# Block products behind gating products, zero matmuls at the head, split column parameters and a later mean square in a two-block kernel

## Chip, cores and metric

The kernel runs on one core of one Trainium2 chip, as one launch. The metric is the device time of the execution in microseconds (us), as the median of the runs shown. Engines are named as the profile names them: PE is TensorE (PEld its weight loads), DVE VectorE, ACT ScalarE, POOL GpSimd, SP SyncE.

## The reference, cut to what matters

Two blocks run one after the other on 256 positions of width 1024, in float32. The first is a mixer of four branches and then a gated FFN with a causal convolution; the second has an S5 branch, an mLSTM branch and a retrieval FFN. The change touches the start of the first block, its FFN, and the preparation of the second block's constants.

```python
def rms_norm(x, g):
    xf = x.astype(jnp.float32)
    y = xf * lax.rsqrt(jnp.mean(xf * xf, axis=-1, keepdims=True) + RMS_EPS)
    return (y * g.astype(jnp.float32)).astype(x.dtype)
...
def first_block(...):
    for l in range(DEPTH):
        h = rms_norm(x, mix_norm_g[l])
        x = x + hybrid_mixer(h, w_in[l], ...)
        h = rms_norm(x, ffn_norm_g[l])
        x = x + conv_glu_ffn(h, w_up[l], ffn_conv_w[l], w_down[l])
    return rms_norm(x, final_norm_g)
...
def conv_glu_ffn(h, w_up, conv_w, w_down):
    up = causal_dwconv(h @ w_up, conv_w)
    gate, val = jnp.split(up, 2, axis=-1)
    return (jax.nn.silu(gate) * val) @ w_down
...
def s5_branch(u, a_re, a_im, log_dt, b_re, b_im, c_re, c_im, d, w_glu, b_glu):
    lam = lax.complex(a_re.astype(f32), a_im.astype(f32))
    dt = jnp.exp(log_dt.astype(f32))[:, None]
    a_bar = jnp.exp(lam * dt)
    b_bar = ((a_bar - 1.0) / lam)[..., None] * lax.complex(b_re.astype(f32), b_im.astype(f32))
    ...
```

The products of `a_bar` with the matrices B and C depend on parameters alone. The kernel multiplies them out for four steps in advance, while the first block's FFN runs.

## The kernel before, in words

Channels lie on partitions, positions along the free axis. Every matrix product keeps float32 precision by three matmuls: weights and activations are each split into a rounded high part and a rest, and `mm3` (L405 to L407) multiplies high by high, high weight by rest, and rest of the weight by high. Weights come in units of eight 128x128 tiles (512 KB). A unit is loaded by SP, its high part `wh` is cast by ACT (L339) and its rest `wl` is subtracted by DVE (L340), up to three units ahead of TensorE.

At the head, the eight channel tiles of X arrive in four loads, with the column parameters `cols` (one 128x286 table) between them. `pre` (L434, L435) scales and splits them into `h`; `square` makes the squares, which POOL sums (L444). The eight z blocks of the rwkv branch are the first products (L405 to L407, out `z`). After the second one, `rstd` (L453) sums the squares over partitions with two matmuls by ones; the scale is applied to z afterwards, in `shift`.

The FFN (`up` and `down`) has 22 steps. `up(i)` makes 48 matmuls into two banks `u`, convolves on ACT and DVE (L1888 to L1890), takes the Silu on ACT (L1891) and multiplies gate by value on POOL (L1892, the gating product; the last three are on DVE). In the next step `split` (L429 on ACT, L430 on DVE) makes `ffnr` from the product, and `down(i - DN)` multiplies it by the down weights with 24 matmuls (L1903 to L1905, out `acc`). So a step has 72 matmuls.

`_prep` is a generator that runs beside the FFN: `tick`, called for each weight unit, lets it issue a little more. Its block products (`paced`, L564) are 48 tensor_tensors of 128x512 on POOL, with a negation at L575 and one at L583. TensorE transposes their results (`pt`, L591), ACT evicts the transposes (L592), and further matmuls (`pk`, L599) follow. Then come eight folds of the mLSTM's matrices: three expands each on POOL (L492) and three small matmuls (`pf`, L639 to L641).

Each engine executes its instructions in its own fixed order. A scheduler derives that order when the program is built; `issue_after(ins)` adds an edge that keeps an instruction behind `ins` on the same engine, and `K.behind` uses that to hold background work behind a unit's cast, split and last matmul:

```python
def step(self, gen, lag):
    if len(self.splits) <= lag:
        return next(gen, None)
    with self.behind(lag):
        return next(gen, None)
```

Of the kernel before, what the change touches and what calls it, by code (L numbers as in the profile page):

```python
# [11 lines left out]
F16 = mybir.dt.float16  # L12
U32 = mybir.dt.uint32
AF = mybir.ActivationFunctionType
ALU = mybir.AluOpType
# [3 lines left out]
P = 128  # L19
D = 1024  # L20
T1 = 256
# [3 lines left out]
NFF = DFF // P  # L25
# [213 lines left out]
class _Space:  # L239


    def __init__(self, t):
        self.t, self.at = t, 0
# [21 lines left out]
class _K:  # L265
    def __init__(self, ctx, tc, I):
        self.tc, self.nc, self.I = tc, tc.nc, I
        self.misc = ctx.enter_context(tc.tile_pool(name="misc", bufs=1))
        self.bigp = ctx.enter_context(tc.tile_pool(name="big", bufs=8))
        self.g8p = ctx.enter_context(tc.tile_pool(name="g8", bufs=3))  # L270
        self.wp = ctx.enter_context(tc.tile_pool(name="w", bufs=4))
        self.dram = ctx.enter_context(tc.tile_pool(name="dram", bufs=1, space=bass.MemoryType.DRAM))
        self.pl = ctx.enter_context(tc.tile_pool(name="pl", bufs=4, space=PSUM))
        self.banks = ctx.enter_context(ExitStack())
        self.pm = self.banks.enter_context(tc.tile_pool(name="pm", bufs=4, space=PSUM))
        self.src = [I["W"][u] for u in range(N_UNITS)] + [I["U"][i] for i in range(NE)] + [I["V"][i] for i in range(NE)]
        self.raw, self.units, self.done = [], {}, 0
        self.at = -1
        self.bg, self.credit, self.rate = [], 0.0, RATE
        self.splits, self.last = [], None  # L280
        self.n = 0

    def name(self, s):
# [64 lines left out]
    def behind(self, lag=0):  # L348
# [4 lines left out]
                s.enter_context(self.tc.issue_after(ins))  # L353
        return s

    def step(self, gen, lag):
        if len(self.splits) <= lag:
            return next(gen, None)
        with self.behind(lag):
            return next(gen, None)  # L360
# [45 lines left out]
        mm(out, wh, al, start=False, stop=False)  # L406
        self.last = mm(out, wl, ah, start=False, stop=last).ins  # L407

    def lin(self, seg, i0, kt, hi, lo, out):

        for k in range(kt):
            wh, wl = self.w(seg, i0 + k)
            self.mm3(out, wh, wl, hi(k), lo(k), k == 0, k == kt - 1)

    def lin_nat(self, seg, hi, lo, outs, tsl, n2=2, kt=8, i0=0):

        mm = self.nc.tensor.matmul
        for k in range(kt):
            b = SEG_BASE[seg] + i0 + k * n2
            wh, wl, j = self.unit(b)  # L420
            rh = wh[:, j:j + n2].rearrange("p a b -> p (a b)")
            rl = wl[:, j:j + n2].rearrange("p a b -> p (a b)")
            for o, s in zip(outs, tsl):
                mm(o, hi(k)[:, s], rh, start=k == 0, stop=False)
                mm(o, hi(k)[:, s], rl, start=False, stop=False)
                mm(o, lo(k)[:, s], rh, start=False, stop=k == kt - 1)
# [18 lines left out]
        else:  # L445
            self.part[1] = s

    def rstd(self):

        nc = self.nc  # L450
        ms = self.ps("ms")[:, :T1]
        for i, s in enumerate(self.part):
            nc.tensor.matmul(ms, self.ones, s, start=i == 0, stop=i == 1)  # L453
        rs = self.misc.tile([P, T2], F32, name=self.name("rs"), tag="rs")
        nc.scalar.activation(rs[:, :T1], ms, AF.Sqrt, bias=self.eps, scale=1.0 / D)
        nc.vector.reciprocal(rs[:, :T1], rs[:, :T1])
        return rs[:, :T1]
# [10 lines left out]
def _prep(K, dump):  # L468

    nc, I, cols = K.nc, K.I, K.cols  # L470
    g = nc.gpsimd
    act, mm, tp = nc.scalar.activation, nc.tensor.matmul, nc.tensor.transpose
    tt, ts, stt = nc.vector.tensor_tensor, nc.vector.tensor_scalar, nc.vector.scalar_tensor_tensor
    EW, CX, TT, ZZ, BX = (K.big(f"s5{i}") for i in range(5))
    ew = EW.a(16, 2, P)
    cx = [CX.a(16, 4, 32) for _ in range(2)]
# [8 lines left out]
    ex = M5.a(3, P)  # L485
    msk = mp[:, 481:513]
    wif = mp[:, 288:480].rearrange("p (a b) -> p a b", b=8)
    wk, wv, rep, tr = mp[:, 0:32], mp[:, 32:64], mp[:, 64:192], [mp[:, 192 + 32 * i:224 + 32 * i] for i in range(3)]

    def expand(w, e, dst):  # L490

        g.tensor_tensor(dst.rearrange("p (a b) -> p a b", b=4), _bc(w[:, 4 * e:4 * e + 4], 1, 32), _bc(msk, 2, 4), ALU.mult)  # L492
# [10 lines left out]
    nc0, dk = (raw[:, 48 + 512 * i:560 + 512 * i].rearrange("p (a b) -> p a b", a=16) for i in range(2))  # L503
    x1, x2, kk = (ZZ.t[:, 2112 + 512 * i:2624 + 512 * i].rearrange("p (a b) -> p a b", a=16) for i in range(3))
    c0 = [TT.t[:, 2048 + 512 * i:2560 + 512 * i].rearrange("p (a b) -> p a b", a=16) for i in range(2)]
# [6 lines left out]
    dt, rho, th, n, r, sn, cs_, hs, den, kr, ki, u, w = v[:13]  # L512
# [46 lines left out]
    def paced(dr, di, xr_, xi, yr, yi):  # L559

        ops = []
        cmul(dr, di, xr_, xi, yr, yi, x1, x2, lambda *z: ops.append(z))
        for n, z in enumerate(ops):
            g.tensor_tensor(*z)  # L564
            if n not in (0, 3):
                yield 0.1

# [4 lines left out]
    for t in (2, 1, 0):  # L572
        yield from paced(bx[0][:, :, t], bx[1][:, :, t], bx[0][:, :, t + 1], bx[1][:, :, t + 1], bar, bai)
    yield from paced(c0[0], c0[1], C[:, 0], C[:, 1], bc(kr), bc(ki))
    g.tensor_scalar(nc0, c0[1], -1.0, None, ALU.mult)  # L575

    def outputs():
        pr, pi_ = c0
        for t in range(4):
            qr, qi = cx[0][:, :, t], cx[1][:, :, t]  # L580
            yield from paced(qr, qi, pr, pi_, bar, bai)
            pr, pi_ = qr, qi
        g.tensor_scalar(cx[1], cx[1], -1.0, None, ALU.mult)  # L583

    def inputs():

# [45 lines left out]
    nc.vector.tensor_reduce(nqk, pr4.rearrange("p (m d) -> p m d", d=4), AX.X, ALU.add)  # L632

    for e in range(8):
        for i in range(3):
            expand(tr[i], e, ex[:, i])
        yield 0.3
        pf = K.ps("pf")
        mm(pf[:, 0:8], ex[:, 0], wif[:, e], start=True, stop=False)  # L639
        mm(pf[:, 0:8], ex[:, 1], wif[:, 8 + e], start=False, stop=True)  # L640
        mm(pf[:, 8:16], ex[:, 2], wif[:, 16 + e], start=True, stop=True)  # L641
        nc.scalar.copy(fold[:, :, e], pf[:, 0:16].rearrange("p (a b) -> p a b", a=2))
# [691 lines left out]
def trainium_kernel(ctx, tc, I, O, dump=None, stop=None):  # L1334
    nc = tc.nc
    K = _K(ctx, tc, I)
    dump = dump or (lambda n, a: None)
    act, stt, tt, ts = nc.scalar.activation, nc.vector.scalar_tensor_tensor, nc.vector.tensor_tensor, nc.vector.tensor_scalar
# [7 lines left out]
    eps = K.misc.tile([P, 2], F32, name="eps")  # L1346
    nc.vector.memset(eps[:, 0:1], 1e-6)
    nc.vector.memset(eps[:, 1:2], 64e-5)
    act(K.misc.tile([P, 2], F32, name="warm"), eps, AF.Copy)
    for a, b in ((0, 1), (1, 2), (2, 4), (4, 8)):  # L1350
        nc.sync.dma_start(xr[:, a:b], I["xT"][:, a:b])
        if a == 0:
            nc.sync.dma_start(cols, I["cols"])
            K.load(1)
        if a == 1:
            K.piece(1)
    nc.sync.dma_start(eye2, I["eye"])
    ident, K.ones, K.iota, K.row0 = eye2[:, :P], eye2[:, P:2 * P], eye2[:, 2 * P:3 * P], eye2[:, 3 * P:]
    K.ident = ident
# [22 lines left out]
    h0, l0 = (lambda k: hi0[:, k]), (lambda k: lo0[:, k])  # L1382
# [39 lines left out]
        act(zp[:, n], zz[:, n, 1:T1 + 1], AF.Copy, scale=omu[:, n:n + 1])  # L1422
        stt(zp[:, n], zz[:, n, 0:T1], col("rw_mu", n), zp[:, n], ALU.mult, ALU.add)

    wait = []
    for j, n in enumerate(RW_ORDER):
        p = K.ps("z")
        K.lin("rw", j * 8, 8, h0, l0, p[:, :T1])
        wait.append((n, p[:, :T1]))
        if j == 1:  # L1430
            rs = K.rstd()
            nrm = K.start(K.normed(xr, COL["mix_norm_g"], rs, hi1, lo1, T1))
        if j:
            for w in wait:
                shift(*w)
            wait = []
# [243 lines left out]
    rw = K.start(rwkv())  # L1680
# [5 lines left out]
    for n in range(4):  # L1686
        p = K.ps("q")
# [59 lines left out]
    for n in range(2):  # L1747
        p = K.ps("u")
# [64 lines left out]
    for b in BR_ORDER[:3]:  # L1813
        g = mg if b == 0 else gc
# [4 lines left out]
        for m in range(4):  # L1819
            p = K.ps("br")  # L1820
# [34 lines left out]
    for n in range(8):  # L1855
        p = K.ps("o")
# [9 lines left out]
    h0, l0 = (lambda k: hi0[:, k]), (lambda k: lo0[:, k, :T1])  # L1866
# [4 lines left out]
    def up(i):  # L1871
        nonlocal rs, nrm, prep
        u, raw = ua[i % 4], i < RAW
        if i == RAW:
            K.finish(nrm)
        ps = [K.ps("u"), K.ps("u")]
        for e in range(2):
            K.lin(f"up{i}", e * 8, 8, h0 if raw else hh, l0 if raw else hl, ps[e][:, :T1])
            if i == 0 and e == 1:
                rs = K.rstd()  # L1880
                nrm = K.start(K.normed(xr, COL["ffn_norm_g"], rs, hi1, lo1, T1))
                prep = K.start(_prep(K, dump))
            for f in (0, 1) if i == 0 and e else (e,) if i else ():
                v, n = ps[f][:, :T1], f * NFF + i
                if raw:
                    tt(uv[:, f], v, rs, ALU.mult)
                    v = uv[:, f]
                act(u[:, f], v, AF.Copy, scale=col("ffn_conv_w", 2 * 44 + n))  # L1888
                stt(u[:, f, 1:], v[:, :T1 - 1], col("ffn_conv_w", 44 + n), u[:, f, 1:], ALU.mult, ALU.add)
                stt(u[:, f, 2:], v[:, :T1 - 2], col("ffn_conv_w", n), u[:, f, 2:], ALU.mult, ALU.add)  # L1890
        act(u[:, 0], u[:, 0], AF.Silu)  # L1891
        (nc.gpsimd.tensor_tensor if i < NFF - 3 else tt)(u[:, 0], u[:, 0], u[:, 1], ALU.mult)  # L1892
        if i > 0 and i <= NFF - 3:
            K.split(*uh[(i - 1) % 4], ua[(i - 1) % 4][:, 0])
        if i >= NFF - 3:
            K.split(*uh[i % 4], u[:, 0])
# [77 lines left out]
```

## Time and profile before

| | |
|---|---|
| median of 3 runs | 1595.97 us (1594.9 to 1597.15) |
| the profiled execution | 1592.86 us |
| its span, first to last instruction | 1591.0 us |
| mean granted TensorE clock | 0.987 |
| TensorE busy | 1535.2 us, 96%, 11661 matmuls |
| VectorE busy | 1146.4 us, 72% |
| ScalarE busy | 832.5 us, 52% |
| GpSimd busy | 237.4 us, 15% |
| the chain that ended last | PE 84%, POOL 7%, DVE 6%, ACT 1% |
| the FFN's gating products on POOL | 305.4 to 505.2 us |

The profile is of one execution. A row of a timeline has the start in us, the duration, the engine, the line, the operation, its output and inputs, the shape and a count; in brackets stands how long the engine had been idle before it and what released it. A row of a wait says which engine and line waited for which, the total in us, how often, and the longest. The granted clock is given as a share of full speed. A duration of a matmul covers its whole passage; matmuls are pipelined, so the time that one costs is the distance between two starts.

### The profile page before, as it was taken

How to read it: one execution, taken by the hardware profiler on the slowest of the kernel's cores; microseconds unless marked ns; L12 is line 12 of the kernel's file. 1: busy time of each engine (PE TensorE's matmuls, PEld its weight loads, DVE VectorE, ACT ScalarE, POOL GpSimd, SP SyncE). 2: the span in 40 equal slices, each digit the busy share in tenths (PEclk: the TensorE clock that was granted, in tenths of full speed). 3: DMA queues.
4: the chain of work that ended last, by engine and by line, in shares of the span. 5: the costliest groups of instructions: out<-in, count | busy, mean ns of one | idle time of the engine just before them, and what ended most of it. 6: DMA issues, size and time to landing. Idle time of an engine off the chain costs nothing.

```text
span 1591.0 us, 29719 instructions
## 1 busy us (share of the span) xinstructions
PE 1535.2 (96%) x11661; PEld 1425.3 (90%) x11661; DVE 1146.4 (72%) x2164; ACT 832.5 (52%) x1439; POOL 237.4 (15%) x254
## 2 busy tenths in 40 slices
PE   7999999987599999999999999999999999999998
PEld 7999899987599997889999999999999888888886
DVE  7765467865477788668899888788999566566664
ACT  7654345744345556555554554544444555555554
POOL 2000000275613002000100431112222000000000
PEclk9999999998899999999999999999999999999999
DMA  7543245544255553245545555555545556556563
GB/s 258 160 136 119 80 133 173 193 146 136 91 174 163 171 166 111 93 134 167 190 159 183 177 158 186 161 161 170 159 160 165 185 194 196 191 195 192 193 197 107
DMA packets 80717, 257.94 MB, mean 162 GB/s; under 512 B 17345, under 2 KB 18881, under 8 KB 80322
## 3 DMA queue, kind: packets, MB, share of 16 engines
q1 hardware_dynamic: 69200, 247.32, 48.3%
q10 hardware_dynamic: 11378, 8.73, 1.9%
q8 instruction: 92, 1.51, 0.4%
q14 instruction: 47, 0.39, 0.1%
HBM read 253.23 MB, written 2.13 MB: 161 GB/s over the span
## 4 chain that ended last, share of the span: by engine, by line
PE 84%; POOL 7%; DVE 6%; ACT 1%; issue 1%; DMA 1%; SPq 0%; ACTq 0%; POOLq 0%; DVEq 0%
PE acc L1297 22%; PE U L405 7%; PE U L407 6%; PE U L406 6%; POOL s L564 4%; PE g L405 3%; PE g L406 3%; PE g L407 3%; DVE wl L340 2%; PE pG L1177 2%; PE u L405 2%; PE u L406 1%; PE u L407 1%; PE q L406 1%; PE q L405 1%; PE q L407 1%
## 5 line engine op out<-in xcount | busy, mean ns | idle before, releaser
L340 DVE TENSOR_TENSOR wl<-wr,wh 128x1024 fp32r<-128x1024 f32 (+1 forms) x469 | 587.4, 1255 | 196.0 <-ACT wh L339 193.1
L339 ACT CAST wh<-wr 128x1024 fp32r<-128x1024 f32 (+1 forms) x469 | 490.6, 1048 | 393.7 <-PE U L406 156.8
L1297 PE MATMUL acc<-wh,wring 128*128 128x512 f32 x1024 | 315.5, 389 | 0.0
L405 PE MATMUL U<-hh,wh 128*128 128x256 f32 x1024 | 292.5, 286 | 0.0
L407 PE MATMUL U<-hh,wl 128*128 128x256 f32 x1024 | 288.1, 281 | 1.5 <-DVE wl L340 1.4
L406 PE MATMUL U<-hl,wh 128*128 128x256 f32 x1024 | 288.3, 282 | 0.0
L1297 PEld LDWEIGHTS acc<-wh,wring 128*128 128x128 f32 x1024 | 192.2, 188 | 40.0
L1297 PE MATMUL acc<-wl,wring 128*128 128x512 f32 x512 | 199.2, 389 | 0.0
L407 PEld LDWEIGHTS U<-hh,wl 128*128 128x128 f32 x1024 | 193.9, 189 | 1.9 <-DVE wl L340 1.9
L405 PEld LDWEIGHTS U<-hh,wh 128*128 128x128 f32 x1024 | 193.4, 189 | 0.0
L406 PEld LDWEIGHTS U<-hl,wh 128*128 128x128 f32 x1024 | 192.5, 188 | 0.0
L1288 ACT ACTIVATE wring<-act 128x256 fp32r<-128x256 f32 x128 | 53.3, 418 | 152.2 <-PE acc L1297 148.7
L1297 PEld LDWEIGHTS acc<-wl,wring 128*128 128x128 f32 x512 | 96.1, 188 | 19.8
L405 PE MATMUL u<-hh,wh 128*128 128x256 f32 x320 | 92.9, 292 | 12.3 <-ACT wh L339 11.6
L1289 DVE SCALAR_TENSOR_TENSOR wring<-act,wring 128x256 fp32r<-128x256 f32 x128 | 54.6, 427 | 60.5 <-PE acc L1297 57.3
L407 PE MATMUL u<-hh,wl 128*128 128x256 f32 x320 | 92.0, 288 | 3.2 <-DVE wl L340 3.2
L406 PE MATMUL u<-hl,wh 128*128 128x256 f32 x320 | 91.4, 287 | 0.0
L1258 POOL TENSOR_TENSOR act<-act,ga 128x16 f32<-128x16 f32 (+31 forms) x77 | 56.5, 733 | 212.4 <-ACT ga L1257 192.3
L444 POOL TENSOR_TENSOR sq<-sq,sq 128x256 f32<-128x256 f32 x18 | 16.0, 888 | 415.4 <-ACT sq L440 415.1
L405 PEld LDWEIGHTS u<-hh,wh 128*128 128x128 f32 x320 | 62.3, 195 | 13.2 <-ACT wh L339 12.0
L405 PE MATMUL g<-hh,wh 128*128 128x256 f32 x256 | 73.8, 288 | 0.0
L406 PE MATMUL g<-hl,wh 128*128 128x256 f32 x256 | 72.0, 281 | 0.0
(643 smaller groups left out, 3411.6 us busy)
## 6 DMA issues: line engine op xcount, KB each, us to landing
wr<-in_W SPq DMA_DIRECT2D x211, 512.0 KB, 3.9
wr<-in_U SPq DMA_DIRECT2D x128, 512.0 KB, 3.9
wr<-in_V SPq DMA_DIRECT2D x128, 512.0 KB, 4.3
s<-in_s5p ACTq DMA_DIRECT2D x1, 1056.0 KB, 6.0
tkc<-in_keysT ACTq DMA_DIRECT2D x1, 1024.0 KB, 6.4
wsA<-in_cst ACTq DMA_DIRECT2D x1, 804.0 KB, 5.2
wsA<-in_rows ACTq DMA_DIRECT2D x1, 640.0 KB, 7.0
s<-s ACTq DMA_DIRECT2D x10, 64.0 KB, 3.0
```

The lines of the kernel that those rows point to most:

```text
L339: a = nc.scalar.copy(hi[:, q], raw[:, q])
L340: b = nc.vector.tensor_tensor(lo[:, q], raw[:, q], hi[:, q].bitcast(F32), ALU.subtract)
L405: mm(out, wh, ah, start=first, stop=False)
L406: mm(out, wh, al, start=False, stop=False)
L407: self.last = mm(out, wl, ah, start=False, stop=last).ins
L444: self.nc.gpsimd.tensor_tensor(self.part[0], self.part[0], s, ALU.add)
L564: g.tensor_tensor(*z)
L1177: mm(o, ring[:, q % 2, e // 2, :, e % 2], ring[:, q % 2, 4 + 2 * w + e // 2, :, e % 2], start=w == 0, stop=w == 1)
L1258: g.tensor_tensor(d[:, :n], d[:, :n], a[:, :n], ALU.mult)
L1288: act(hi, w, AF.Copy, scale=1.0 / 16384)
L1289: stt(lo, w, 1.0 / 16384, hi.bitcast(F32), ALU.mult, ALU.subtract)
L1297: mm(acc[t][c], w[:, q], v[:, 4 * c:4 * c + 4].rearrange("p a b -> p (a b)"), start=False, stop=i == NE - 1 and len(vs) == 1, skip_group_c ...
```

## The change

It has four parts. The last gating product on POOL is kept as `K.pace`, and the block products and expands of `_prep` are issued behind it on POOL. A tile of zeros, `idle`, is written by POOL, and `spin` issues matmuls of it on TensorE: eight before the first z product, and 3, 6 and 3 within the first z block. `cols` is loaded in two transfers, the first 8 columns early and the rest behind the loads of units 0 to 1, ahead of `eye`. The mean square `rstd` is taken in the middle of the third z block, into a bank of its own, and the shifts of the first three z blocks follow that block together.

```diff
-        self.splits, self.last = [], None
+        self.splits, self.last, self.pace = [], None, None
...
+    def paced(self):
+
+        return ExitStack() if self.pace is None else self.tc.issue_after(self.pace)
...
-    def lin(self, seg, i0, kt, hi, lo, out):
+    def lin(self, seg, i0, kt, hi, lo, out, between=None):
 
         for k in range(kt):
+            if between:
+                between(k)
             wh, wl = self.w(seg, i0 + k)
             self.mm3(out, wh, wl, hi(k), lo(k), k == 0, k == kt - 1)
+
+    def spin(self, n):
+
+        p = self.pm_("spin")
+        for _ in range(n):
+            self.nc.tensor.matmul(p, self.idle[:, :P], self.idle, start=True, stop=True)
...
-    def rstd(self):
+    def rstd(self, bank=None):
...
-        ms = self.ps("ms")[:, :T1]
+        ms = (bank or self.ps)("ms")[:, :T1]
...
         for n, z in enumerate(ops):
-            g.tensor_tensor(*z)
+            with K.paced():
+                g.tensor_tensor(*z)
...
-    g.tensor_scalar(nc0, c0[1], -1.0, None, ALU.mult)
+    with K.paced():
+        g.tensor_scalar(nc0, c0[1], -1.0, None, ALU.mult)
...
-        g.tensor_scalar(cx[1], cx[1], -1.0, None, ALU.mult)
+        with K.paced():
+            g.tensor_scalar(cx[1], cx[1], -1.0, None, ALU.mult)
...
     for e in range(8):
-        for i in range(3):
-            expand(tr[i], e, ex[:, i])
+        with K.paced():
+            for i in range(3):
+                expand(tr[i], e, ex[:, i])
...
+    K.idle = K.misc.tile([P, 512], F16, name="idle", tag="ix")
+    nc.gpsimd.memset(K.idle, 0.0)
     act(K.misc.tile([P, 2], F32, name="warm"), eps, AF.Copy)
+    K.spin(8)
...
-            nc.sync.dma_start(cols, I["cols"])
+            nc.sync.dma_start(cols[:, :8], I["cols"][:, :8])
             K.load(1)
         if a == 1:
             K.piece(1)
+    K.load(2)
+    nc.sync.dma_start(cols[:, 8:], I["cols"][:, 8:])
     nc.sync.dma_start(eye2, I["eye"])
...
-    wait = []
+    wait, rs = [], None
     for j, n in enumerate(RW_ORDER):
         p = K.ps("z")
-        K.lin("rw", j * 8, 8, h0, l0, p[:, :T1])
+        def between(k):
+            nonlocal rs
+            if j == 0 and 0 < k < 4:
+                K.spin((3, 6, 3)[k - 1])
+            if j == 2 and k == 4:
+                rs = K.rstd(K.pm_)
+
+        K.lin("rw", j * 8, 8, h0, l0, p[:, :T1], between)
         wait.append((n, p[:, :T1]))
-        if j == 1:
-            rs = K.rstd()
+        if j == 2:
             nrm = K.start(K.normed(xr, COL["mix_norm_g"], rs, hi1, lo1, T1))
-        if j:
+        if j > 1:
...
-        (nc.gpsimd.tensor_tensor if i < NFF - 3 else tt)(u[:, 0], u[:, 0], u[:, 1], ALU.mult)
+        prod = (nc.gpsimd.tensor_tensor if i < NFF - 3 else tt)(u[:, 0], u[:, 0], u[:, 1], ALU.mult)
+        K.pace = prod.ins if i < NFF - 3 else None
```

The lines of the changed kernel have other numbers: L564 is L577 there, L1892 is L1919, L492 is L504, L405 to L407 are L409 to L411, L639 to L641 are L655 to L657.

POOL's order in the FFN, from behind gating product 4 to product 5 and the three after it. `s` holds the S5 block products, `ffn` the gating products. Before:

```order
L564 TENSOR_TENSOR s_3382<-s_3381 128x16x32
L564 TENSOR_TENSOR s_3381<-s_3382,s_3380 128x512 x2
L564 TENSOR_TENSOR s_3382<-s_3381 128x16x32
L564 TENSOR_TENSOR s_3381<-s_3382,s_3380 128x512 x2
L564 TENSOR_TENSOR s_3382<-s_3381 128x16x32
L564 TENSOR_TENSOR s_3381<-s_3381,s_3380 128x512 x2
L564 TENSOR_TENSOR s_3380<-s_3381 128x512
L564 TENSOR_TENSOR s_3381<-s_3381,s_3380 128x512 x2
L564 TENSOR_TENSOR s_3380<-s_3381 128x512
L575 TENSOR_SCALAR s_3381<-s_3380 128x512
L564 TENSOR_TENSOR s_3381<-s_3380 128x512 x2
L1892 TENSOR_TENSOR ffn_2985<-ffn_2985 128x256 x4
```

The same place on POOL after the change, gating products 4, 5 and 6:

```order
L1919 TENSOR_TENSOR ffn_3012<-ffn_3012 128x256
L577 TENSOR_TENSOR s_3408<-s_3409,s_3407 128x512 x2
L577 TENSOR_TENSOR s_3409<-s_3408 128x16x32
L577 TENSOR_TENSOR s_3408<-s_3409,s_3407 128x512 x2
L1919 TENSOR_TENSOR ffn_3012<-ffn_3012 128x256
L577 TENSOR_TENSOR s_3409<-s_3408 128x16x32
L577 TENSOR_TENSOR s_3408<-s_3409,s_3407 128x512 x2
L577 TENSOR_TENSOR s_3409<-s_3408 128x16x32
L1919 TENSOR_TENSOR ffn_3012<-ffn_3012 128x256
L577 TENSOR_TENSOR s_3408<-s_3409,s_3407 128x512 x2
L577 TENSOR_TENSOR s_3409<-s_3408 128x16x32
L577 TENSOR_TENSOR s_3408<-s_3409,s_3407 128x512 x2
```

Sixteen block instructions stood between product 4 and product 5 before, and now five; behind products 4 to 13 there are 5, 4, 5, 4, 6, 4, 5, 4, 5 and 4 of them, and the large negation (L598) stands behind product 14.

POOL's order at the end of the FFN's gating products. `ml` holds the expands of the folds. Before, behind the product that was fourth from the last:

```order
L492 TENSOR_TENSOR ml_3383<-ml_3383 128x128 x9
L1892 TENSOR_TENSOR ffn_2985<-ffn_2985 128x256
L492 TENSOR_TENSOR ml_3383<-ml_3383 128x128 x8
L1892 TENSOR_TENSOR ffn_2985<-ffn_2985 128x256
L492 TENSOR_TENSOR ml_3383<-ml_3383 128x128 x7
```

After the change:

```order
L504 TENSOR_TENSOR ml_3410<-ml_3410 128x128 x6
L1919 TENSOR_TENSOR ffn_3012<-ffn_3012 128x256
L504 TENSOR_TENSOR ml_3410<-ml_3410 128x128 x9
L1919 TENSOR_TENSOR ffn_3012<-ffn_3012 128x256
L504 TENSOR_TENSOR ml_3410<-ml_3410 128x128 x12
```

Three expands stood ahead of gating product 0 before and now stand with the others; six, nine and twelve of them follow products 15, 16 and 17.

TensorE's order where fold 2 (`pf`) stands, at the end of a `down` step (`acc`). Before:

```order
L1903 MATMUL acc_3287<-ffnr_2986,wh_5144 128x256
L1904 MATMUL acc_3287<-ffnr_2986,wh_5144 128x256
L1905 MATMUL acc_3287<-ffnr_2986,wl_5145 128x256
L639 MATMUL pf_5273<-ml_3383 128x8
L640 MATMUL pf_5273<-ml_3383 128x8
L641 MATMUL pf_5273<-ml_3383 128x8
L405 MATMUL u_5265<-hh_3282,wh_5182 128x256
```

After the change:

```order
L1933 MATMUL acc_3311<-ffnr_3013,wl_5295 128x256
L1931 MATMUL acc_3312<-ffnr_3013,wh_5294 128x256
L1932 MATMUL acc_3312<-ffnr_3013,wh_5294 128x256
L655 MATMUL pf_5300<-ml_3410 128x8
L656 MATMUL pf_5300<-ml_3410 128x8
L409 MATMUL u_5292<-hh_3309,wh_5209 128x256
L657 MATMUL pf_5300<-ml_3410 128x8
```

The fold stands eight `acc` matmuls further back, and its third matmul behind the first of the next `up` step.

## Rows read from the trace of the kernel before

**Rows 1.** the page: busy time, share and instructions of each engine

```profile
PE 1535.2 (96%) x11661; PEld 1425.3 (90%) x11661; DVE 1146.4 (72%) x2164; ACT 832.5 (52%) x1439; POOL 237.4 (15%) x254
```

**Rows 2.** TensorE's waits, 285 to 520 us: total, times, longest

```profile
PE pt L591 <- ACT s L592: 15.9, 2, 14.4
PE u L405 <- ACT wh L339: 11.6, 2, 9.5
```

**Rows 3.** windows: length, busy (count) per engine, clock, DMA share, GB/s

```profile
342.90:372.60 29.70, 16.33 (x95) 15.33 (x94) 12.65 (x16) 8.77 (x14) 23.25 (x20) 0.71 0.24 76
400.40:431.00 30.60, 14.19 (x105) 13.57 (x104) 11.72 (x13) 9.71 (x18) 24.30 (x16) 0.78 0.22 69
```

**Rows 4.** timeline of ACT around the two windows

```profile
343.87 0.41 ACT L429 CAST ffnr<-ffn 128x256 fp32r<-128x256 f32 x1 [10.81 <-POOL ffn L1892]
425.53 0.40 ACT L429 CAST ffnr<-ffn 128x256 fp32r<-128x256 f32 x1 [16.65 <-POOL ffn L1892]
```

**Rows 5.** timeline of POOL, gating products and pairs of block products

```profile
335.75 3.90 POOL L564 TENSOR_TENSOR s<-s,s 128x512 f32<-128x512 f32 x2
343.11 0.72 POOL L1892 TENSOR_TENSOR ffn<-ffn 128x256 f32<-128x256 f32 x1
354.94 2.06 POOL L564 TENSOR_TENSOR s<-s,s 128x512 f32<-128x512 f32 x2
365.38 0.72 POOL L1892 TENSOR_TENSOR ffn<-ffn 128x256 f32<-128x256 f32 x1
371.84 1.58 POOL L1892 TENSOR_TENSOR ffn<-ffn 128x256 f32<-128x256 f32 x1 [5.74 <-DVE ffn L1890]
424.77 0.72 POOL L1892 TENSOR_TENSOR ffn<-ffn 128x256 f32<-128x256 f32 x1
```

**Rows 6.** timeline of DVE, operands of product 4 and weight splits

```profile
332.46 0.47 DVE L1890 SCALAR_TENSOR_TENSOR ffn<-u,cols,ffn 128x254 f32<-128x254 f32 x1
332.85 5.89 DVE L340 TENSOR_TENSOR wl<-wr,wh 128x1024 fp32r<-128x1024 f32 x3
369.57 1.21 DVE L340 TENSOR_TENSOR wl<-wr,wh 128x1024 fp32r<-128x1024 f32 x1
```

**Rows 7.** timeline of PE, half speed, full speed, a group of transposes

```profile
349.04 0.41 PE L405 MATMUL u<-hh,wh 128*128 128x256 f32 x1
349.25 0.41 PE L406 MATMUL u<-hl,wh 128*128 128x256 f32 x1
353.38 0.28 PE L1904 MATMUL acc<-ffnr,wh 128*128 128x256 f32 x1
353.50 0.28 PE L1905 MATMUL acc<-ffnr,wl 128*128 128x256 f32 x1
390.75 0.60 PE L591 MATMUL pt<-eye,s 128*128 128x128 f32 x4
```

**Rows 8.** window of PE alone: length, busy (count), clock, DMA share, GB/s

```profile
345.30:352.10 6.80, 5.49 (x24) 0.50 0.45 144
```

**Rows 9.** POOL's groups by line and form, 285 to 510 us

```profile
L564 POOL TENSOR_TENSOR s<-s,s 128x512 f32<-128x512 f32 x28 | 36.6, 1325 | 8.1 <-DVE s L531 7.1
```

**Rows 10.** timeline of POOL, product 16 and the expands behind it

```profile
485.54 1.58 POOL L1892 TENSOR_TENSOR ffn<-ffn 128x256 f32<-128x256 f32 x1 [0.56 <-DVE ffn L1890]
487.27 1.36 POOL L492 TENSOR_TENSOR ml<-ml 128x128 f32<-128x128 f32 x3
```

**Rows 11.** timeline of PE, a fold's first matmuls

```profile
483.42 0.28 PE L639 MATMUL pf<-ml 128*128 128x8 f32 x2
```

**Rows 12.** timeline of PE and DVE at the head

```profile
4.62 0.58 PE L405 MATMUL z<-h,wh 128*128 128x256 f32 x1 [4.62 <-ACT wh L339]
13.31 0.41 PE L405 MATMUL z<-h,wh 128*128 128x256 f32 x1
15.97 0.70 PE L453 MATMUL ms<-sq,eye 128*128 128x256 f32 x2 [1.51 <-POOL sq L444]
17.79 2.36 DVE L340 TENSOR_TENSOR wl<-wr,wh 128x1024 fp32r<-128x1024 f32 x2 [2.65 <-ACT wh L339]
```

## Prediction, made before the changed kernel was run

> **What bounds the kernel now.** I began with the page's busy line: TensorE works for 96% of the span [rows 1], so only stretches in which it waits or runs slowly can give anything back. Second came TensorE's waits over the first FFN, 285 to 520 us: two waits of the transposes `pt` for their eviction on ACT (15.9 us together, one of 14.4) and two waits of `u` for the weight cast `wh` (11.6, one of 9.5) [rows 2]. Third, two windows around these waits: in 29.70 us TensorE does 95 matmuls at a mean clock of 0.71, and in 30.60 us 105 at 0.78 [rows 3]. Last, the timelines of ACT, POOL and DVE inside them, which say why.
>
> ACT stands still because its next instruction, the cast of the gated product (L429), waits for the product on POOL (L1892): 10.81 us before 343.87, 16.65 before 425.53 [rows 4]. What stands behind that cast in ACT's order, `wh` casts and evictions, waits too, though it needs nothing from POOL. POOL is late because block products (L564) stand ahead: product 4 had its operands when DVE ended L1890 at 332.46 + 0.47 = 332.93 [rows 6] and began at 343.11 [rows 5]. Behind it the order has 16 block instructions before product 5, which begins at 365.38. Product 10 begins at 424.77, behind the second such run [rows 5]. So the critical resource is POOL's place in line, not its busy share.
>
> The clock makes it dearer. At full speed the matmuls stand 353.50 − 353.38 = 0.12 us apart (0.119 over many), after the first hole 349.25 − 349.04 = 0.21 (0.213) [rows 7]; that stretch shows a granted clock of 0.50, the 1.2 GHz level, for 6.80 us [rows 8]. TensorE had idled before each fall.
>
> **The change, part by part.**
> *Block products behind the gating product.* Nothing of them is added or removed: 48 tensor_tensors and the scalings stay on POOL, now 4 to 6 after each of products 4 to 13. If every product were in time, the first window would need 95 × 0.119 = 11.3 of its 29.70 us and gain 18.4. The second, with 90 matmuls and 15 transposes of 0.60/4 = 0.15 us [rows 7], would need 13.0 of 30.60 and gain 17.6. Together **36.0 us**.
>
> *What POOL then needs.* A step of the FFN is 72 matmuls, 72 × 0.119 = 8.6 us; five take 43. In the five steps from product 4 the new order has 24 block instructions. At the mean of their rows, about 1.35 us (the commoner form has 1.33, the rarer a little more) [rows 9], with a product of 1.1 (between its 0.72 and 1.58 [rows 5]), that is 24 × 1.35 + 5 × 1.1 = 37.9: it fits, and costs 0. At the contended price, two in 3.90 = 1.95 each beside DVE's `wl` splits (335.75) where two take 2.06 elsewhere (354.94) [rows 5], and products of 1.58, it is 54.7: 11.7 too long. That pair of ends is the bound. Contention acts only while DVE splits weights: three splits of 1.21 us [rows 6] in a step of 8.6, a share of 0.42. I take 0.42 × 11.7 = **4.9 us** lost.
>
> DVE suffers in the same overlap: three splits took 5.89 us, 1.96 each, beside block products, and 1.21 alone [rows 6]. The Trainium skill, page "SBUF — State Buffer", section "Who interferes with whom", says that the two engines share one port pair as an exclusive lock, and that a DVE instruction with two SBUF inputs contends with a GpSimd instruction that reads SBUF. The trace agrees as to 1.96 against 1.21. By that rule spreading the products over more steps spreads the collisions over more splits, which speaks against the change; it is rival B.
>
> *Expands behind the gating product.* Here the change adds a wait. In POOL's new order the expands of folds 2 to 4 stand behind product 16, which is ready at 485.54 and takes 1.58; the first three expands behind it take 1.36 [rows 10], so fold 2 is ready at about 488.6. TensorE reaches it at 483.42 + 8 × 0.119 = 484.4 (eight down matmuls further back than before) [rows 11]. It waits 4.2 us, and every up product stands behind that wait on TensorE. Fold 5 behind product 17 has the same shape with seven matmuls: between 0 and 2.2 us, taken as 1.4. **5.6 us** lost. The least is 0, if products come earlier against TensorE; the most is 4.2 + 2.2 and a stretch at half speed, 6.80 × (1 − 0.119/0.213) = 3.0, together 9.4 [rows 8].
>
> *The head.* Before, the first triple begins at 4.62, matmuls at 13.31 still last 0.41 us as at half speed, and the mean-square matmul holds z for 1.51 us before 15.97 [rows 12]. Eighteen z matmuls run so; at full speed they would save 18 × 0.094 = 1.7. With the mean square moved to the third block, that wait is gone too: at most 3.2. But the third block needs unit 2's `wl`, whose split ends no sooner than 17.79 + 1.2 = 19.0 [rows 12], where TensorE now needs it at some 19.6. That leaves 0.6, and I add 0.4 for a chain that starts a little sooner: **1.0 us** gained, between 0 and 3.2. The zero matmuls have no row. By the nearest, 0.41 for 256 columns at half speed [rows 7], one of 512 columns lies between 0.4 and 0.8; eight from about 1.1 end between 4.3 and 7.5, against a first triple at 4.62. I take the near end since TensorE waits for inputs in those microseconds anyway. The far end would delay the chain by 2.9, which TensorE's waits before 15.97 absorb; if not, the head gain is 0.
>
> *At nothing.* The split column load, the later `eye` and the zero tile's memset: TensorE reads `eye` first at the mean square, past 15.97, and POOL idles in the first microseconds. Uncovered, each would delay the head by an issue and end its gain. The later shift of the first z blocks lies on DVE and ACT beside the next z block's matmuls.
>
> *Sum.* 36.0 − 4.9 − 5.6 + 1.0 = 26.5 us. The profiled execution took 1592.86 us, so 1566.4; the median of the runs, 1595.97, lies 3.1 above it: **1569.5 us**.
>
> **The rivals.**
> *B, the overlap with DVE holds every step.* All block products at 1.95 us (11.7 lost) and the folds at their worst (9.4): 36.0 − 11.7 − 9.4 + 1.0 = 15.9, giving 1580.1. For it: 3.90 and 5.89 [rows 5, 6]. Against: the 28 block products of the commoner form cost 1.33 in the mean [rows 9], with DVE at its splits for part of them.
>
> *C, everything fits.* POOL keeps up and the folds' expands arrive in time: 36.0 + 1.0 to 36.0 + 3.2, or 1557 to 1559. Against it: 488.6 and 484.4 come from rows and leave little doubt of some wait.
>
> *D, the hole only moves.* Some other late block product keeps ACT, or the order does not act on the chip as it reads: about 1596. Against it: POOL runs in its written order in the trace.
>
> *E, slower.* POOL becomes the limit of every step, and TensorE, idle once a step, falls to 1.2 GHz each time. A step on POOL at contended prices is 4.6 × 1.95 + 1.58 = 10.6, with 0.7 to hand over 11.3, and 3.0 for the half speed: 14.3. The step without waits is 8.6 and a tenth of the eight groups of transposes, 8 × 0.60 / 10 = 0.5 [rows 7]: 9.1. Ten steps lose 52, with folds 57.6, against 37.0 gained: 20.6 slower, 1616.6. It decides from (37.0 − 5.6)/10 = 3.1 us lost in each step, a step of 12.2. For it: the clock fell after each hole [rows 3, 8]. Against: POOL alone does not reach 12.2 even at its worst price, so TensorE must idle and slow down in every step, while weights already split ahead let it work on through a short lateness.
>
> **How the numbers follow.** My forecast 0.60, B 0.18, C 0.13, D 0.04, E 0.05. About 0.2%, 3.2 us, is what a measurement of this kernel can tell from no change (its three runs lie between 1594.9 and 1597.15). Forecast, B and C are all faster than that: 0.91; D is the same: 0.04; E slower: 0.05. The range goes from C's best, 1557, to B's 1580.1 with the head at nothing (1581) and the 1.2 us by which a run exceeded the median, rounded up: 1583. D and E lie outside.
>
> **What the changed profile would show.** Right: no wait of ACT's L429 cast on POOL over some 3 us; gating products 8.6 to 11 us apart from product 4 to 14; TensorE's waits of `pt` and of `u` for `wh` near nothing in the first FFN, and the clock at 1.00 from 340 us to the FFN's end; a new wait of `pf` on POOL's expand, 4 to 6 us in all; z matmuls 0.12 apart by 9 or 10 us and no wait of `ms` over 1 us. B would show in a `wl` split mean near 1.9 and block products near 1.95 throughout that stretch. The forecast would be wrong by its fold term if no `pf` wait stands there, by its contention term if the steps take 8.6 or over 11 us, and by its main term if ACT still stands for 10 us behind a gating product. E would show as a clock near 0.8 over the whole FFN.

## The result and the profile after

The changed kernel takes 1571.19 us in the median of four runs (1570.34 to 1575.34), against 1595.43 for the kernel before (1593.64 to 1597.15). The ratio is 0.9853, with a 95% interval from 0.9832 to 0.9874: 24.2 us faster, and 1.7 us above the forecast of 1569.5. Its profiled execution spans 1568.5 us, 22.5 less than before.

First, the page's busy line after; TensorE now works for 98% of the span, against 96% [rows 1].

```profile
PE 1536.9 (98%) x11681; PEld 1423.6 (91%) x11681; DVE 1162.1 (74%) x2164; ACT 832.4 (53%) x1439; POOL 249.3 (16%) x255
```

TensorE's waits after, up to 520 us (total, times, longest):

```profile
PE pf L655 <- POOL ml L504: 6.1, 2, 5.1
PE acc L1933 <- DVE wl L340: 1.6, 2, 1.1
...
PE u L409 <- DVE ffn L1917: 1.2, 2, 0.7
PE pt L606 <- ACT s L607: 1.1, 1, 1.1
...
PE u L411 <- DVE wl L340: 0.8, 1, 0.8
```

Both big waits of [rows 2] are gone: `pt` waits 1.1 us where it waited 15.9, and `u` waits for no `wh`. The new wait is the one of `pf` on the expands. The windows from gating product 3 to 14 and from 14 to 18 (length, busy and count of PE, PEld, DVE, ACT and POOL, clock, DMA share, GB/s), before and then after:

```profile
326.59:465.38 138.79, 108.40 (x857) 106.59 (x856) 75.29 (x108) 53.63 (x87) 82.51 (x61) 0.89 0.41 127
465.38:504.49 39.11, 39.11 (x337) 39.11 (x335) 32.87 (x81) 19.39 (x39) 17.64 (x29) 1.00 0.59 190
```

```profile
326.45:432.59 106.14, 102.73 (x865) 101.82 (x864) 89.27 (x108) 53.28 (x88) 90.48 (x61) 1.00 0.54 166
432.59:483.17 50.58, 44.26 (x343) 43.48 (x341) 36.37 (x82) 20.81 (x41) 24.93 (x33) 0.90 0.45 147
```

Here lies the whole account of the two profiled executions. Up to product 3 both kernels are level (326.59 and 326.45). From 3 to 14 the change gains 138.79 − 106.14 = 32.7 us, and the clock there is 1.00 where it was 0.89. From 14 to 18 it loses 50.58 − 39.11 = 11.5, at a clock of 0.90. What follows product 18 is 1.2 us shorter. Together 0.1 + 32.7 − 11.5 + 1.2 = 22.5. The stretches are cut at starts of products on POOL, so the work in them is not quite the same: the first holds 865 matmuls after against 857 before, the second 343 against 337. At 0.12 us apiece that is 1.0 and 0.7 us of the two figures.

POOL after, at the places of [rows 5] and [rows 10] (product 4 with its block products, product 5, then product 14, the large negation, product 15 and the first expands):

```profile
332.57 1.58 POOL L1919 TENSOR_TENSOR ffn<-ffn 128x256 f32<-128x256 f32 x1 [0.82 <-DVE ffn L1917]
334.12 4.02 POOL L577 TENSOR_TENSOR s<-s,s 128x512 f32<-128x512 f32 x2
338.22 1.35 POOL L577 TENSOR_TENSOR s<-s 128x512 f32<-128x512 f32 x1
339.65 3.96 POOL L577 TENSOR_TENSOR s<-s,s 128x512 f32<-128x512 f32 x2
343.76 1.58 POOL L1919 TENSOR_TENSOR ffn<-ffn 128x256 f32<-128x256 f32 x1
...
432.59 1.58 POOL L1919 TENSOR_TENSOR ffn<-ffn 128x256 f32<-128x256 f32 x1 [2.73 <-DVE ffn L1917]
434.15 6.34 POOL L598 TENSOR_SCALAR s<-s 128x2048 f32<-128x2048 f32 x1
445.70 0.73 POOL L1919 TENSOR_TENSOR ffn<-ffn 128x256 f32<-128x256 f32 x1 [5.22 <-DVE s L566]
446.40 3.77 POOL L504 TENSOR_TENSOR ml<-ml 128x128 f32<-128x128 f32 x6
```

Product 4 begins at 332.57 instead of 343.11, and five block instructions stand behind it. ACT's waits for gating products, 300 to 500 us, in each kernel:

```profile
ACT ffnr L429 <- POOL ffn L1892: 64.6, 14, 16.6
```

```profile
ACT ffnr L441 <- POOL ffn L1919: 22.7, 14, 3.6
```

ACT stands 22.7 us at that cast instead of 64.6, and never over 3.6.

### The profile page after: what moved, and what is told of

Read it like the earlier page. It is cut to its first block, busy times and chain, and to the rows that moved or that the text cites. A ratio compares the mean times of both kernels' runs of the same rounds, so it can differ in the third digit from the quotient of the medians.

```text
span 1568.5 us, 29762 instructions
## 1 busy us (share of the span) xinstructions
PE 1536.9 (98%) x11681; PEld 1423.6 (91%) x11681; DVE 1162.1 (74%) x2164; ACT 832.4 (53%) x1439; POOL 249.3 (16%) x255
## 4 chain that ended last, share of the span: by engine, by line
PE 82%; DVE 9%; POOL 4%; ACT 2%; issue 2%; DMA 1%; ACTq 0%; SPq 0%; DVEq 0%; POOLq 0%
PE acc L1313 22%; PE U L409 7%; PE U L411 7%; PE U L410 7%; DVE wl L340 4%; PE g L409 3%; PE g L410 3%; PE g L411 3%; PE pG L1193 2%; POOL s L577 2%; PE u L409 1%; PE u L410 1%; PE u L411 1%; PE q L410 1%; PE q L409 1%
## 5 line engine op out<-in xcount | busy, mean ns | idle before, releaser
L340 DVE TENSOR_TENSOR wl<-wr,wh 128x1024 fp32r<-128x1024 f32 (+1 forms) x469 | 595.7, 1273 | 197.2 <-ACT wh L339 193.9
L409 PE MATMUL U<-hh,wh 128*128 128x256 f32 x1024 | 292.5, 286 | 0.0
L411 PE MATMUL U<-hh,wl 128*128 128x256 f32 x1024 | 288.1, 281 | 1.4 <-DVE wl L340 1.4
L411 PEld LDWEIGHTS U<-hh,wl 128*128 128x128 f32 x1024 | 193.9, 189 | 1.9 <-DVE wl L340 1.9
L409 PEld LDWEIGHTS U<-hh,wh 128*128 128x128 f32 x1024 | 193.5, 189 | 0.0
L409 PE MATMUL u<-hh,wh 128*128 128x256 f32 x320 | 91.7, 288 | 1.4 <-DVE ffn L1917 1.2
L411 PE MATMUL u<-hh,wl 128*128 128x256 f32 x320 | 90.9, 285 | 0.8 <-DVE wl L340 0.8
L409 PE MATMUL g<-hh,wh 128*128 128x256 f32 x256 | 73.8, 288 | 0.0
L411 PE MATMUL g<-hh,wl 128*128 128x256 f32 x256 | 71.9, 281 | 0.0
```

Source lines behind the costliest of these rows:

```text
L340: b = nc.vector.tensor_tensor(lo[:, q], raw[:, q], hi[:, q].bitcast(F32), ALU.subtract)
L409: mm(out, wh, ah, start=first, stop=False)
```

## The experiments

**The pacing alone, the head as before.** The edits to the head are undone, the four uses of `paced` stay.

```diff
-    K.spin(8)
...
-            nc.sync.dma_start(cols[:, :8], I["cols"][:, :8])
+            nc.sync.dma_start(cols, I["cols"])
...
-            if j == 2 and k == 4:
-                rs = K.rstd(K.pm_)
...
+        if j == 1:
+            rs = K.rstd()
```

> The pacing alone, with the head as it was before. Theory H0 (the head's edits are worth nothing, since the z products wait for weight transfers in any case): 1570 to 1573 us, within 0.2% of the changed kernel's 1571.2. Theory H1 (the head is worth 1 to 3 us, as the prediction's head term and its upper bound say): 1572 to 1574.5. Under both, the FFN's waits are those of the changed kernel: no 14 us wait of pt, one wait of about 5 us of pf on the expand.

Measured: 1572.23 us, ratio 0.9859 (0.9842 to 0.9876); the first matmuls `pf` wait the same 6.1 us, and one third matmul another 0.7. The pacing carries the gain. H0 and H1 both hold 1572.2.

**The head alone.**

```diff
-        K.pace = prod.ins if i < NFF - 3 else None
+        K.pace = None
```

> The head's edits alone, with block products and expands issued as before. Both holes of the FFN stay (ACT's cast of ffnr waits 10 to 17 us for the gating product). H0: 1594 to 1597 us, the same as before (first q matmul at 37.5 us in the trace, as in both kernels). H1: 1592 to 1594, with the first q matmul 1 to 3 us earlier.

Measured: 1592.73 us, ratio 0.9992 (0.998 to 1.0003). TensorE's waits are those of before:

```profile
PE pt L606 <- ACT s L607: 15.8, 2, 14.4
PE u L409 <- ACT wh L339: 11.4, 2, 9.3
```

Both holes stand. The median lies 1.8 us below that of before, within H1, but the interval includes no change. The first q matmul of the trace starts at 36.67, 0.8 us earlier than before: not H0's 37.5, and not quite H1's full microsecond.

**Expands free.**

```diff
-        with K.paced():
-            for i in range(3):
-                expand(tr[i], e, ex[:, i])
+        for i in range(3):
+            expand(tr[i], e, ex[:, i])
```

> The changed kernel, but the folds' expands are not kept behind the last gating product. Theory F (fold 0 waits because its expands stand behind gating product 15): fold 0's expands run early, the pf wait of 5.1 us and the half-speed stretch behind it go, and the time falls by 8 to 11 us to 1560 to 1563. Theory N (product 15 itself is late, because the 6.3 us negation on POOL holds DVE's small products and with them the convolution): product 15 still comes at about 445 us, ACT's cast still waits for it, and TensorE waits somewhere else; gain under 4 us, 1567 to 1571.

Measured: 1563.21 us, ratio 0.9796 (0.978 to 0.9812), 8.0 us under the changed kernel. Product 15 is as late as it was, yet of the waits of `pf` only one of 1.6 us and one of 0.2 are left:

```profile
PE pf L654 <- POOL ml L504: 1.6, 1, 1.6
```

```profile
431.24 1.58 POOL L1918 TENSOR_TENSOR ffn<-ffn 128x256 f32<-128x256 f32 x1 [2.73 <-DVE ffn L1916]
432.79 6.34 POOL L598 TENSOR_SCALAR s<-s 128x2048 f32<-128x2048 f32 x1
444.36 0.75 POOL L1918 TENSOR_TENSOR ffn<-ffn 128x256 f32<-128x256 f32 x1 [5.22 <-DVE s L566]
```

So most of the loss is theory F, with a gain at the lower end of its 8 to 11. Not all of F came true: a stretch of slow clock is still there, a mean of 0.77 from 445 to 460 us. Theory N's lateness is there too: product 15 begins 13.1 us behind product 14.

**The negation on ACT.**

```diff
-        with K.paced():
-            g.tensor_scalar(cx[1], cx[1], -1.0, None, ALU.mult)
+        nc.scalar.mul(cx[1], cx[1], -1.0)
```

> The changed kernel, but the negation of 128x2048 is done by ACT, not by POOL; the expands stay behind the gating products. Theory N: DVE's 3.6 us product of 128x16 falls to about 0.2, product 15 comes some 3 us earlier against TensorE, the pf wait falls from 5.1 to 2 us or less, and 3 to 6 us are gained: 1565 to 1568. Theory F: product 15 is late for its own chain (up, convolution, Silu), the pf wait stays above 4 us, and the time stays within 0.2% of 1571.

Measured: 1566.78 us, ratio 0.9824 (0.9808 to 0.9841), 4.4 us under the changed kernel, with `pf` waits of 1.3 us at the longest. The row that explains it is one small product on DVE, first in the changed kernel, then here:

```profile
435.18 3.60 DVE L564 TENSOR_TENSOR s<-s 128x16 f32<-128x16 f32 x1
```

```profile
431.73 0.70 DVE L564 TENSOR_TENSOR s<-s 128x16 f32<-128x16 f32 x1
```

Beside the negation on POOL (434.15 to 440.49) this product of 128x16 took 3.60 us. With the negation on ACT, where it is over at 430.04, the same product took 0.70, now beside gating product 14 on POOL. The convolution stands behind it on DVE, so product 15 came late. Here product 15 begins 10.2 us behind product 14, not 13.1, and the 2.9 us between are those between 3.60 and 0.70:

```profile
430.82 1.58 POOL L1918 TENSOR_TENSOR ffn<-ffn 128x256 f32<-128x256 f32 x1 [2.73 <-DVE ffn L1916]
441.02 0.73 POOL L1918 TENSOR_TENSOR ffn<-ffn 128x256 f32<-128x256 f32 x1 [8.62 <-DVE s L569]
```

**Thin block products.** Each block product covers a sixteenth of its elements, so the S5 constants are left out of the computation.

```diff
             with K.paced():
-                g.tensor_tensor(*z)
+                g.tensor_tensor(*(a[:, :1] if hasattr(a, "shape") else a for a in z))
```

> The changed kernel, but each of the 48 block products covers 128x32 instead of 128x512 (their tiles are cleared beforehand on POOL), so most of their elements are left out and the S5 constants are not computed; order, edges, expands and the big negation stay. What remains beside the FFN is POOL's order without POOL's load. The prediction's contention term says 4.9 us in the steps from product 4 on: from gating product 3 to 14 the trace should take 101 to 102 us instead of the changed kernel's 106.1, weight splits 1.2 instead of 1.5 us, and the time 1565 to 1568. Theory B, the overlap holds every step: 94 to 96 us there and 1558 to 1561. Theory C, the overlap costs nothing: 105 to 106 us there and 1570 to 1572.

Measured: 1566.29 us, ratio 0.9829 (0.9811 to 0.9846), 4.9 us under the changed kernel. From product 3 to 14, as in the windows above:

```profile
326.06:426.39 100.33, 100.33 (x854) 100.33 (x853) 67.07 (x105) 54.25 (x87) 33.30 (x61) 1.00 0.55 174
```

These 100.33 us against 106.14 put POOL's load at 5.8 us of the stretch: a little over the prediction's term and half of B's. TensorE is busy throughout, where it was busy for 102.73 of 106.14 us: it waited 1.2 us for the convolution, 1.1 for a `wl` split and 1.1 for an eviction. The window here holds 11 matmuls fewer, so about 1.3 of the 5.8 us are the cut, and the medians' 4.9 are the better figure. The weight splits from 325 to 435 us (count, busy and mean ns), in the changed kernel and here:

```profile
L340 DVE TENSOR_TENSOR wl<-wr,wh 128x1024 fp32r<-128x1024 f32 x35 | 57.3, 1649 | 2.7 <-ACT wh L339 2.3
```

```profile
L340 DVE TENSOR_TENSOR wl<-wr,wh 128x1024 fp32r<-128x1024 f32 x36 | 48.5, 1349 | 21.9 <-ACT wh L339 21.9
```

**Gating products on DVE, otherwise the kernel before.**

```diff
-        (nc.gpsimd.tensor_tensor if i < NFF - 3 else tt)(u[:, 0], u[:, 0], u[:, 1], ALU.mult)
+        tt(u[:, 0], u[:, 0], u[:, 1], ALU.mult)
```

> The kernel before, but all gating products run on DVE, so that nothing on POOL stands ahead of them; the block products stay where they were, in one run on POOL. Theory Q (the holes came from the products' place in POOL's line): both holes go, ACT's cast of ffnr no longer waits over 3 us, and with 19 products of some 0.4 us more on DVE and the block products beside its splits the time is 1558 to 1568. Theory R (ACT or the transposes were held by the block products themselves, whoever makes the gating products): a wait of pt over 8 us stays and the time is above 1580.

Measured: 1567.0 us, ratio 0.9836 (0.9818 to 0.9854). The block products run on POOL in one piece, as before, and no wait of `pt` is left; ACT's cast never waits over 2.8 us (its wait from 300 to 500 us, then TensorE's up to 520):

```profile
ACT ffnr L429 <- DVE ffn L1892: 16.9, 12, 2.8
```

```profile
PE u L405 <- DVE ffn L1890: 5.1, 3, 3.1
```

So the holes came from the gating products' place in POOL's line and not from the block products being late for TensorE. DVE pays: from 325 to 435 us its splits take 1.80 us in the mean, and TensorE waits 5.1 us for the convolution.

**Expands free and the negation on ACT.** Both edits above together.

> The changed kernel with both edits: the folds' expands free and the negation on ACT. If the two waits are separate (expands behind product 15; product 15 late through the negation), the gains of 8.0 and 4.4 us add in part: 1558 to 1561. If the second only mattered through the first, 1562 to 1564, as with the expands free alone.

Measured: 1559.32 us, ratio 0.9788 (0.9768 to 0.9809), 11.9 us under the changed kernel. The gains add, 8.0 and 3.9, though one of the five runs took 1566.45. From product 14 to 18:

```profile
432.70:470.73 38.03, 38.03 (x328) 38.03 (x326) 33.14 (x81) 19.74 (x40) 19.77 (x28) 1.00 0.57 195
```

The 50.58 us are now 38.03, at full clock. Before the change they were 39.11, with nine matmuls more in the window, so nothing of the loss is left. This is the lowest median of the study.

**No zero matmuls.**

```diff
-    K.spin(8)
...
-            if j == 0 and 0 < k < 4:
-                K.spin((3, 6, 3)[k - 1])
```

> The changed kernel without the matmuls of zeros; the split column load and the later mean square stay. H0 (the head waits for weight transfers): the z matmuls up to about 14 us last 0.41 again, the first q matmul still starts between 36 and 38 us, and the time is 1569 to 1573, the changed kernel's. H1 (the clock at the head counts): the first q matmul at 38.5 us or later and 1573 to 1575.

Measured: 1570.62 us, ratio 0.9855 (0.9839 to 0.987), the changed kernel's time. Without zeros the z matmul at 13.00 lasts 0.41 us, with them the one at 12.93 lasts 0.28 (first this kernel, then the changed one):

```profile
13.00 0.41 PE L410 MATMUL z<-h,wh 128*128 128x256 f32 x1
```

```profile
12.93 0.28 PE L410 MATMUL z<-h,wh 128*128 128x256 f32 x1
```

The first q matmul comes no later without them: at 35.95, against 37.47 in the changed kernel's profile. So the zeros do bring the matmuls to full speed earlier, and no gain from it can be seen, which is H0; a microsecond would not stand out from intervals of this width.

**The best kernel with the old head.** Block products paced, expands free, negation on ACT, the head as before.

> The block products behind the gating products, expands free, negation on ACT, and the head as it was before. H0 (the head's edits are worth nothing): 1558 to 1561 us, like the same kernel with the new head (1559.3). H1 (they are worth 1 to 3 us): 1560.5 to 1563, above it in most of its runs.

Measured: 1561.07 us, ratio 0.9782 (0.9768 to 0.9796). Its median is 1.7 us above that of the kernel with the new head, its ratio, to the runs beside it, 0.0006 below: inconclusive in time. In the traces the first q matmul starts at 38.58, against 35.56 with the new head, and product 0 at 307.15 against 304.29.

**The columns in one transfer**, otherwise the changed kernel.

```diff
-            nc.sync.dma_start(cols[:, :8], I["cols"][:, :8])
+            nc.sync.dma_start(cols, I["cols"])
...
-    nc.sync.dma_start(cols[:, 8:], I["cols"][:, 8:])
```

> The changed kernel with the column parameters in one transfer again (143 KB ahead of the first weights). Theory W (the head is bound by the stream of weights, and the split lets weights through earlier): in the first 37.5 us the transfers fall to about 259 GB/s, the first q matmul starts at 37.5 us or later, and the time is 1571 to 1574. Theory S (the zero matmuls or the mean square give the head what it gains): about 272 GB/s and a first q matmul at 35.5 to 36.7 us, as in the other kernels with the new head, and 1569 to 1571.5.

Measured: 1574.98 us, ratio 0.9872 (0.9855 to 0.9888). By its trace the first q matmul starts at 36.3 us at 270 GB/s, as theory S has it; the time is higher than either theory allows. In its profile the extra lies elsewhere: product 0 begins at 303.32, earlier than the changed kernel's 304.56, from product 14 (431.40) to 18 (484.32) it takes 52.9 us against 50.6, and what follows product 18 takes 1089.7 us against 1085.3. The trace speaks against theory W, and the time is not explained by the head.

**The split of the columns alone in the old head**, with the pacing. The edit is shown against the kernel with the pacing alone; it includes the earlier load of unit 2 that goes with the split.

```diff
-            nc.sync.dma_start(cols, I["cols"])
+            nc.sync.dma_start(cols[:, :8], I["cols"][:, :8])
...
+    K.load(2)
+    nc.sync.dma_start(cols[:, 8:], I["cols"][:, 8:])
```

> The pacing with the old head, and of the head's edits the split of the column parameters (with unit 1's load and the later eye) alone. Theory W: about 272 GB/s in the first 37.5 us, the first q matmul at 35.5 to 36.7 us, 1569 to 1571.5. Theory S: about 259 GB/s, the first q matmul at 37.5 us or later, 1571.5 to 1574.

Measured: 1571.24 us, ratio 0.9857 (0.9841 to 0.9874), with the first q matmul at 36.65 and 262 GB/s. The time and the matmul are W's, the rate is nearer S's, and the run before spoke against W: inconclusive.

## Why the prediction was right, and where its steps were not

**The cause was right.** ACT's in-order queue stood behind late gating products. Taking the products off POOL removes the holes as well as moving them forward does, which leaves little room for another cause.

**The recoverable 36.0 us were some 2.5 too few.** With POOL's load nearly gone, the stretch from product 3 to 14 takes 100.3 us, 38.5 less than before. The stretch is cut at starts of products on POOL and not of matmuls, so a microsecond or two of this is the cut; the rest was not traced to a row.

**The contention term, 4.9, was right in size, in part by luck.** The thin products gave 4.9 us in the medians and 5.8 in the stretch, and rival B's full 11.7 did not occur. The price was read well: the 48 block products took 1.60 us in the mean (28 of 1.508 and 20 of 1.760), between the 1.35 and 1.95 of the prediction and at its share of 0.42. But the working counts 24 block instructions in five steps, and the new order spreads 46 over ten. Over all ten the same sum is 46 × 1.95 + 10 × 1.58 − 86 = 19.5 too long, and 0.42 of it 8.2. So the term stood for half of the stretch and came out near the whole. The rule of the Trainium skill named in the prediction (page "SBUF — State Buffer", section "Who interferes with whom") is borne out by the splits: 1.65 us in the mean beside full block products, 1.35 beside thin ones. That speaks against the change, but for 5 us only. That section of the Trainium skill calls the pair an exclusive lock, and says of DVE's two-port modes that it is held for the whole instruction. By the profile's records the large negation on POOL did not hold DVE's small product that long: the product ended at 438.78, the negation at 440.49.

**The fold term, 5.6, was the step that failed: it measured 11.5.** The prediction said that "the expands of folds 2 to 4 stand behind product 16" and that TensorE waits 4.2 us there. TensorE waits at fold 0, behind product 15, and fold 5 waits 1.0 (1.4 predicted):

```profile
448.02 0.60 PE L655 MATMUL pf<-ml 128*128 128x8 f32 x2 [5.10 <-POOL ml L504]
472.19 0.39 PE L655 MATMUL pf<-ml 128*128 128x8 f32 x2 [1.04 <-POOL ml L504]
```

The waits of `pf` came to 6.1 us in all, near the 5.6, but at another fold. Two things were not in the sum. First, product 15 was taken to be in time, and folds 0 and 1 behind it were given no wait. In the new order the large negation stands directly behind product 14, runs beside DVE's small products of `_prep` and holds one of them for 3.6 us, and the convolution for product 15 stands behind those. Second, TensorE falls to half speed behind a wait of 5.1 us. From 449.90 to 454.59 its matmuls stand 0.21 apart; the prediction had such a stretch, 3.0 us, only in the bound, of 9.4, which was passed. By its own factor, 1 − 0.119/0.213, the slow stretch from 448.02 to 455.77 costs an estimated 3.4 us. With TensorE's idle 6.3 us of the window (50.58 − 44.26) and the 0.7 of the cut that makes 10.4 of the 11.5. With the expands free 8.0 us are back, with the negation on ACT as well all of them.

**The head, 1.0, remains between 0 and 2 us.** The first q matmul starts at 37.5 in the profiles of before and after alike, but the changed kernel's profile is the odd one: the seven others with the new head or most of it have it at 35.6 to 36.7, and the three others with the old head at 37.9 to 38.6. In medians the head is worth 1.8 us alone, 1.0 on the pacing and 1.7 on the best kernel, no one of these clear of noise. The reason given in the prediction, z matmuls at full speed, is not borne out: without zeros the first q matmul is as early and the time the same within noise. Which of the other edits carries the head's gain stays open.

**The errors nearly cancelled.** The middle stretch gave 32.7 where 36.0 − 4.9 = 31.1 was forecast, the folds cost 11.5 and not 5.6, the head gave 0.1 in this execution and what follows product 18 another 1.2: 22.5 where 26.5 was the sum. That the time came within 1.7 us of the forecast is luck in part. Two of the announced signs failed: the clock did not stay at 1.00 (0.90 from product 14 to 18), and the gating products from 4 to 14 stand 7.4 to 11.9 us apart, not 8.6 to 11. Of the rivals, E's price was not near: steps from product 4 to 14 took 10.0 us each in the mean (332.57 to 432.59), under the 12.2 from which it decides.

## What to carry to other kernels

Look at what stands behind a waiting instruction on its own engine: products that came late from an engine busy for 15% of the time cost some 36 us, because another engine's queue stood behind them. When background work is put behind a pacing point, ask of each consumer whether it is near: here the block products, which TensorE reads later, could be paced, and the expands, which it reads next, could not. And price the collision of a long instruction with the small ones of the engine that shares its time, not only the long one's own duration.

## What the hardware showed unexpectedly

A DVE product of 128x16, 0.16 us by itself, lasted 3.60 us beside a POOL negation of 128x2048, and the negation in turn lasted 6.34 us where it took 5.4 before. The same form later in the changed kernel, with nothing on POOL, and the negation on ACT, where it lasts 1.92 us:

```profile
442.21 0.16 DVE L564 TENSOR_TENSOR s<-s 128x16 f32<-128x16 f32 x1
```

```profile
428.12 1.92 ACT L597 ACTIVATE s<-s 128x2048 f32<-128x2048 f32 x1 [0.19 <-POOL s L577]
```

In that run the small product took 0.70 us beside gating product 14 on POOL and ended with it, at 432.43 and 432.40. So beside this short POOL product it was held to the end, and beside the negation, as the profile records it, not: there DVE went on at 438.71, with a split of the usual 1.21 us next, 1.8 us before the negation's end.

How much slow clock follows a wait could not be read from the wait's length. Behind the 5.1 us of fold 0 TensorE ran at half speed for some 6 us (449.54 to 455.77). With the expands free a wait of 1.6 us also left matmuls 0.21 apart, from 448.57 to 453.26, and a mean clock of 0.77 from 445 to 460 us, while behind the changed kernel's wait of 1.0 us at 472.19 the clock stayed at 1.00.
